# Low parts of two mixers' weights made by GpSimd and an accumulating transfer, in an order chosen from six rules

## The chip, the cores and the metric

One core of a Trainium2 chip runs the whole kernel. The metric is the device time of one execution in microseconds. TensorE (PE in the profile) multiplies, VectorE (DVE), ScalarE (ACT) and GpSimd (POOL) work on tiles, and SyncE (SP) issues the loads.

## The reference

Two layers of a transformer over 512 tokens of width 1024, batch 1, in float32. Each layer has a mixer, a cross attention to 256 memory tokens and a gated feed-forward, each behind a norm and followed by another norm that is added to the stream.

```python
for layer in range(2):
    h = rms_norm(x, g[0])
    y = even_mixer(h, ...) if layer % 2 == 0 else diff_mixer(h, ...)
    x = x + rms_norm(y, g[1])
    y = memory_cross_attention(rms_norm(x, g[2]), mem_n, wq, wk, wv, wo)
    x = x + rms_norm(y, g[3])
    y = swiglu(rms_norm(x, g[4]), wg, wu, wd)
    x = x + rms_norm(y, g[5])
```

The mixer of layer 0 has 8 heads with a forget gate ("fox") and 8 heads in two groups that add compressed, selected and windowed attention ("nsa"). The mixer of layer 1 has 8 differential heads of width 128. Each mixer begins with projections of `h` by one wide weight matrix and ends with an output matrix.

## The kernel before

Every product that needs float32 precision is made from three products in the faster type float32r: each operand is split into a rounded part `hi` and the rest `lo`, and `mm` adds hi*hi, hi*lo and lo*hi in PSUM. So each weight that comes from memory is split once before its use. `wunit` does that for 128x1024 elements: SP loads 512 KB into one of 3 `raw` buffers, then `split` lets ScalarE write `hi` (a copy that rounds) and VectorE write `lo` (raw minus hi). `hi` and `lo` lie in 8 buffers called `w`, four pairs. A unit with `rows` has a gain for each row multiplied in and goes another way (`wq`, and the keys and values of the memory).

The mixers: `mixer0` projects values, keys and compressed keys for all four blocks of 128 tokens, then works through the fox heads in pairs (`fox_proj`, `fox_units`), the queries of each nsa group (`nsa_q`), the compressed scores (`nsa_cmp`, products with 32 columns) and the two groups' attention (`nsa_units`). `mixer1` projects two heads at a time (`proj`: values, queries, keys, each by two units of weights) beside the attention of the two heads before. `last_heads` runs beside the last group of heads in both layers: `first_heads` multiplies the first six 128-row pieces of the heads' output by the output matrix (two times three units, one for each 512 columns, and two more units kept for the last two pieces), and `chain` takes each block of 128 tokens through the last two pieces, the norm, the memory attention with `wq` and `wo`, and the next norm. `wo` is two units, which need two of the four pairs. Softmax rows are scaled by GpSimd (`tensor_scalar`), and GpSimd computes the power of each norm on one column.

Nothing is issued where the code stands. Each call goes to a `Plan`, which notes the instruction, its tiles and a price in nanoseconds. `order` then runs a list scheduler forward through all instructions (`forward`), computes from the result how late each may be (`backward`), takes that as the new priorities, and repeats. The run with the shortest modelled end gives the order in which every engine's queue is written, the loads on SP included. `ALPHA` and `BETA` say when an engine should wait for a more urgent instruction that is soon ready, and `AHEAD` says how far an instruction may take a buffer out of turn.

Of the kernel before, what the change touches and what calls it, by code (L numbers as in the profile page):

```python
# [11 lines left out]
F32 = mybir.dt.float32  # L12
F32R = mybir.dt.float32r
I32 = mybir.dt.int32
AF = mybir.ActivationFunctionType
ALU = mybir.AluOpType
# [3 lines left out]
P = 128  # L20
# [15 lines left out]
KA = 6  # L36
PLAIN = 2
HALF_ROWS = 115
ROWS = slice(0, DH), slice(DH, P)
ORDER = 0, 4, 5, 6, 7, 1, 8, 9, 10, 11, 12, 13, 2, 3  # L40
FILL0, FILL1, STAGE, LATE = 0.0, 1.2, 2.0, 30
# [48 lines left out]
class Plan:  # L90
# [3 lines left out]
    LAT = dict(tt=0, ts=197, tv=230, tg=200, st=265, ss=160, sv=145, sg=170, vt=235, vs=198, vv=127, vg=203,  # L94
               gt=190, gs=190, gv=60, gg=110)
    BLOCK = 8
    ROUNDS = 14
    WINDOW = 4096 / 1.2
    FREE = 150.0
    NEAR, FEW = 10000.0, 12  # L100
    AHEAD, EARLY, RING = 50000.0, 60000.0, 8
    ALPHA, BETA = 1.0, 2.0

    def __init__(self, nc):
        self.nc = nc
# [73 lines left out]
    def price(self, eng, method, args, kw, aps):  # L179
        n = max([self.free(a) for a in aps] + [1])  # L180
        if method == "dma_start":
            size = 1
            for _, k in aps[0].ap:
                size *= k
            return size * 4 / 360.0
        if eng == "tensor":
            if method == "transpose":
                return 109.0
            c = self.free(args[2]) / 2.4
            return max(25.0, (13.0 if c > 100 else 6.5) + (c if args[2].dtype == F32R else 4 * c))  # L190
        half = HALF_ROWS if eng in ("scalar", "vector") and n > 100 and aps[0].ap[0][1] == DH else 0
        if eng == "scalar":
            extra = sum(isinstance(kw.get(k), bass.AP) for k in ("bias", "scale", "accum_out"))
            return (52 if aps[1].space == PSUM else 95) + 0.83 * n + 93 * extra + half
        if eng == "vector":
            psum = any(a.space == bass.MemoryType.PSUM for a in aps)
            n = n + 62 * sum(isinstance(v, bass.AP) and self.free(v) == 1 for v in args[2:3])
            if method == "reciprocal":
                return 60 + 8 * n
            if method in ("tensor_copy", "tensor_scalar", "memset") and not psum:  # L200
                return 65 + 0.52 * n
            return 65 + 1.04 * n + half
        if eng == "gpsimd":
            if method == "tensor_tensor":
                return 260 + 200 * n
            if method == "memset":
                return 30 + 0.84 * n
            return (322 if len(aps) > 3 else 222) + 0.84 * n
        raise ValueError(method)

    def order(self):
        ops = self.ops
        n = len(ops)
        self.eng = [o["eng"] for o in ops]
        self.succ = [[] for _ in range(n)]
        for i, o in enumerate(ops):
            for j in o["deps"]:
                self.succ[j].append(i)
        best = None
        prio = [float(o["prio"]) for o in ops]  # L220
        for _ in range(self.ROUNDS):
            for i, o in enumerate(ops):
                prio[o["group"]] = min(prio[o["group"]], prio[i])
            prio = [prio[o["group"]] for o in ops]
            for k, o in enumerate(self.firsts):
                prio[o["group"]] = k - 1e9
            r = self.forward(prio, self.AHEAD - best[0] if best else math.inf)
            if best is None or r[0] < best[0]:
                best = r
            prio = self.backward(r)  # L230
        self.span, self.at, self.fin, out = best[:4]
        return out

    def backward(self, run):

        span, at, fin, out, reuse = run
        ops, eng, n = self.ops, self.eng, len(self.ops)
        pred = [list(o["deps"]) for o in ops]
        for j, i in reuse:
            pred[i].append(j)  # L240
        left = [0] * n
        for p in pred:
            for j in p:
                left[j] += 1
        engines = ("tensor", "vector", "scalar", "gpsimd", "sync")
        ready = {e: [] for e in engines}
        busy = {e: 0.0 for e in engines}
        ev = [(0.0, i, i) for i in range(n) if not left[i]]
        heapq.heapify(ev)
        at2 = [0.0] * n  # L250
        late = [0.0] * n
        seq = n
        while ev:
            now = ev[0][0]
            while ev and ev[0][0] <= now + 1e-9:
                i = heapq.heappop(ev)[2]
                if i >= 0:
                    heapq.heappush(ready[eng[i]], (-fin[i], i))
            for e in engines:
                h = ready[e]  # L260
                while h and busy[e] <= now + 1e-9:
                    i = heapq.heappop(h)[1]
                    cost = ops[i]["cost"]
                    end = now + cost
                    if ops[i]["dma"]:
                        end += 2000
                    late[i] = -end
                    busy[e] = now + (60 if ops[i]["dma"] and e != "sync" else cost)
                    heapq.heappush(ev, (busy[e], seq, -1))
                    seq += 1  # L270
                    for j in pred[i]:
                        left[j] -= 1
                        f = eng[j]
                        at2[j] = max(at2[j], end + self.LAT.get(f[0] + e[0], 100.0))
                        if not left[j]:
                            heapq.heappush(ev, (max(at2[j], now), j, j))
        return late

    def forward(self, prio, far):

        ops, eng, succ = self.ops, self.eng, self.succ
# [111 lines left out]
        while done < n:  # L393
# [21 lines left out]
            while again:  # L415
                again = False
                for e, heap in ready.items():
                    while heap and busy[e] <= now + 1e-9:
# [12 lines left out]
                        cost = o["cost"]  # L431
                        if o["dma"]:
                            at[i] = now
                            busy[e] = now + 60
                            gen = max(gen, now + 100, ring.pop(0)) + 460
                            dma = max(dma, gen + 640) + cost
                            fin = dma + 950
                            ring.append(fin)
                        else:
                            if e == "tensor":  # L440
                                while now >= (window + 1) * self.WINDOW:
                                    share = worked / self.WINDOW
                                    warm = share > 0.82 or warm and share > 0.42
                                    window, worked = window + 1, 0.0
                                begin = max(now, begin + o["load"] * (1 if warm else 2))
                                if not warm:
                                    cost *= 2
                                worked += cost
                                at[i] = begin
                            else:  # L450
                                at[i] = now
                            busy[e] = fin = at[i] + cost
# [20 lines left out]
class Trunk:  # L473
    def __init__(self, ctx, tc, a, out):
        self.tc, self.a, self.out = tc, a, out
        self.nc = Plan(tc.nc)
        self.sb = ctx.enter_context(tc.tile_pool(name="sb", bufs=1))
        self.ps = ctx.enter_context(tc.tile_pool(name="ps", bufs=1, space=PSUM))
        self.loads = []


    def bank(self):
# [15 lines left out]
    def wunit(self, pieces, n, where=None, rows=None, raw=None):  # L498

        nc = self.nc  # L500
        raw = raw or self.tile([P, 1024], F32, "raw", 3)
        for dst, src in pieces:
            self.loads.append(nc.sync.dma_start(dst(raw), src))
        if where is None:
            hi, lo = [self.tile([P, 1024], F32R, "w", 8) for k in ("hi", "lo")]
        else:
            hi, lo = where()
        if rows is None:
            self.split(hi[:, :n], lo[:, :n], raw[:, :n])
        else:  # L510
            c = n // len(rows)
            for k, f in enumerate(rows):
                s = slice(k * c, (k + 1) * c)
                self.split(hi[:, s], lo[:, s], raw[:, s], f)
        return hi, lo
# [499 lines left out]
    def ffn(self, l, x, ops):  # L1015
# [2 lines left out]
        blocks = {"A11": [t[:, 0:4, 0:256] for t in hT], "A12": [t[:, 4:8, 0:256] for t in hT],  # L1018
                  "A22": [t[:, 4:8, 256:512] for t in hT], "S3": [t[:, 0:4, 256:512] for t in hT],
                  "S1": S[1], "S2": S[2], "S4": S[4]}  # L1020
        groups = [list(range(c, min(c + 3, NCH))) for c in range(0, NCH - 1, 3)]
        groups[-1].append(NCH - 1)
        acts = {}
# [114 lines left out]
    def mixer0(self, x0):  # L1138
# [78 lines left out]
        kcT, kcL, vcBD = self.compress(zst)  # L1217

        oS = self.oS_tiles(2)
        fox, nq, pc = {}, {}, {}  # L1220

        def fox_proj(p):
# [297 lines left out]
    def mixer1(self, x, blocks):  # L1520
# [70 lines left out]
            proj_qk(0, wf, tb, 1)  # L1591
        late.pop()()
        oS = self.oS_tiles(NT)

        def subln(ops, dst):

# [127 lines left out]
```

## Time and profile before

| | |
|---|---|
| median of 3 runs | 1386.26 us (1384.96 to 1386.47) |
| profiled execution | 1385.17 us |
| its span, first to last instruction | 1383.4 us |
| busy: TensorE, VectorE, ScalarE, GpSimd | 1352.8, 1114.9, 861.1, 200.0 us |
| transfers | 132.29 MB, all issued by SP |

Busy time of an engine is the time in which at least one of its instructions was under way; matmuls overlap in the pipeline, so a busy TensorE is one that never ran dry. All instructions stand under one source line (L470, where the planner issues them), so rows are told apart by their tiles: `w<-raw,w` is the making of a low part from `raw` and the high part.

### The profile page before, as it was taken

What the parts mean: (1) busy time and instruction counts of PE and PEld (TensorE: products, weight loads), DVE (VectorE), ACT (ScalarE), POOL (GpSimd) and SP (SyncE); (2) the same over time, 40 slices, a digit from 0 to 9 for tenths busy, and PEclk for the clock granted to TensorE, in tenths of its full rate; (3) what the DMA queues carried; (4) which work ended last, traced back from release to release, by engine and by line L of the source; (5) the groups of instructions that cost most, each with busy time, mean ns of one, the idle gap of its engine ahead of it and who ended that gap; (6) DMA issues with size and microseconds to landing.
All of it is one profiled execution on the core that took longest, in us unless ns stands there. A gap on an engine that the chain in (4) does not pass through costs nothing.

```text
span 1383.4 us, 25460 instructions
## 1 busy us (share of the span) xinstructions
PE 1352.8 (98%) x9443; PEld 1247.4 (90%) x9443; DVE 1114.9 (81%) x2485; ACT 861.1 (62%) x1954; POOL 200.0 (14%) x307
## 2 busy tenths in 40 slices
PE   7999999999899999999999999999999999999998
PEld 6788998888799999999989999988889999999997
DVE  6767899589897887788786788795999788778876
ACT  5758879588766355345455778795886545434542
POOL 2102223343300000000010132321430000000000
PEclk9999999999999999999999999999999999999999
DMA  7252112412234343323432231253223424332431
GB/s 224 67 154 63 32 32 77 137 47 77 62 96 119 92 122 107 93 80 119 128 116 62 77 106 49 77 169 106 77 62 92 122 85 130 95 104 77 123 107 61
DMA packets 150444, 132.29 MB, mean 96 GB/s; under 512 B 6928, under 2 KB 134096, under 8 KB 150320
## 3 DMA queue, kind: packets, MB, share of 16 engines
q1 hardware_dynamic: 150320, 130.67, 31.0%
q8 instruction: 74, 1.21, 0.4%
q14 instruction: 50, 0.41, 0.1%
HBM read 126.26 MB, written 4.19 MB: 94 GB/s over the span
## 4 chain that ended last, share of the span: by engine, by line
PE 84%; DVE 8%; ACT 2%; issue 2%; DMA 2%; POOL 1%; SPq 0%; POOLq 0%; DVEq 0%; ACTq 0%
PE ps L470 84%; DVE q L470 2%; DVE u L470 1%; DVE x L470 1%; DVE w L470 1%; POOL c L470 1%; DVE pt L470 1%; ACT q L470 1%; DMA raw<-in_ffn_wu_dram 1%; ACT junk L470 1%; DVE c L470 1%; DVE hTlo L470 1%; DMA x<-in_x_dram 0%; DMA raw<-in_od_w_in_dram 0%; ACT u L470 0%
## 5 line engine op out<-in xcount | busy, mean ns | idle before, releaser
L470 PE MATMUL ps<-hThi,w 128*128 128x256 f32 (+1 forms) x1664 | 338.4, 292 | 1.7 <-ACT hThi L470 1.2
L470 PE MATMUL ps<-w,hThi 128*128 128x256 f32 (+2 forms) x1280 | 282.9, 316 | 1.6 <-ACT hThi L470 1.6
L470 PEld LDWEIGHTS ps<-hThi,w 128*128 128x128 f32 x1664 | 272.1, 192 | 8.8 <-ACT hThi L470 2.1
L470 PE MATMUL ps<-hTlo,w 128*128 128x256 f32 (+1 forms) x832 | 242.2, 292 | 2.4 <-DVE hTlo L470 2.4
L470 PE MATMUL ps<-pt,u 128*128 128x512 f32 (+3 forms) x1126 | 231.4, 339 | 0.4 <-DVE pt L470 0.3
L470 PEld LDWEIGHTS ps<-w,hThi 128*128 128x128 f32 x1280 | 210.4, 192 | 14.3 <-ACT hThi L470 2.3
L470 PEld LDWEIGHTS ps<-pt,u 128*128 128x128 f32 (+1 forms) x1126 | 173.9, 174 | 28.5 <-DVE pt L470 1.0
L470 PE MATMUL ps<-w,hTlo 128*128 128x256 f32 (+2 forms) x640 | 199.4, 313 | 0.0
L470 DVE TENSOR_TENSOR w<-raw,w 128x512 fp32r<-128x512 f32 (+2 forms) x193 | 170.3, 887 | 31.6 <-ACT w L470 27.4
L470 PE MATMUL ps<-u,w 128*128 128x256 f32 x1440 | 192.9, 283 | 0.4 <-DVE ps L470 0.4
L470 ACT ACTIVATE w<-raw 128x512 fp32r<-128x512 f32 (+2 forms) x193 | 148.5, 786 | 68.8 <-DMA raw<-in_ffn_wg_dram 24.7
L470 ACT ACTIVATE q<-ps 128x256 f32<-128x256 f32 (+5 forms) x282 | 118.3, 428 | 112.1 <-PE ps L470 96.3
L470 PE MATMUL ps<-u 128*128 128x512 f32 (+4 forms) x806 | 185.8, 348 | 1.1 <-ACT u L470 0.6
L470 PEld LDWEIGHTS ps<-u,w 128*128 128x128 f32 x1440 | 181.8, 192 | 1.4 <-DVE ps L470 0.9
L470 DVE TENSOR_TENSOR u<-ps,u 128x512 f32<-128x512 f32 (+6 forms) x278 | 149.6, 545 | 39.8 <-PE ps L470 20.8
L470 PEld LDWEIGHTS ps<-hTlo,w 128*128 128x128 f32 x832 | 159.3, 192 | 6.1 <-DVE hTlo L470 3.2
L470 ACT ACTIVATE u<-ps 64x256 fp32r<-64x256 f32 (+5 forms) x277 | 120.5, 442 | 51.1 <-PE ps L470 47.6
L470 PEld LDWEIGHTS ps<-u 128*128 128x128 f32 (+1 forms) x806 | 129.4, 184 | 19.8 <-ACT u L470 1.2
L470 POOL TENSOR_TENSOR c<-c,mhalf 128x1 f32<-128x1 f32 (+1 forms) x68 | 60.9, 897 | 511.5 <-DVE c L470 502.6
L470 ACT ACTIVATE w<-q 128x512 fp32r<-128x512 f32 x160 | 99.9, 629 | 48.4 <-PE ps L470 22.7
L470 PEld LDWEIGHTS ps<-w,hTlo 128*128 128x128 f32 x640 | 122.4, 192 | 6.6 <-DVE hTlo L470 0.2
L470 DVE TENSOR_TENSOR w<-q,w 128x512 fp32r<-128x512 f32 x160 | 107.9, 686 | 21.2 <-ACT w L470 20.5
(153 smaller groups left out, 1917.6 us busy)
## 6 DMA issues: line engine op xcount, KB each, us to landing
raw<-in_ffn_wg_dram SPq DMA_DIRECT2D x44, 512.0 KB
raw<-in_ffn_wu_dram SPq DMA_DIRECT2D x44, 512.0 KB
raw<-in_ffn_wd_dram SPq DMA_DIRECT2D x44, 512.0 KB
raw<-in_od_w_in_dram SPq DMA_DIRECT2D x24, 512.0 KB
raw<-in_ev_w_in_dram SPq DMA_DIRECT2D x16, 512.0 KB
u<-in_sandwich_g_dram SPq DMA_DIRECT2D x10, 512.0 KB
x<-in_x_dram SPq DMA_DIRECT2D x8, 512.0 KB
raw<-in_ev_w_out_dram SPq DMA_DIRECT2D x8, 512.0 KB
```

The lines of the kernel that those rows point to most:

```text
L470: getattr(getattr(self.nc, self.eng[i]), method)(*args, **kw)
```

## The change

The planner's constants, prices and search, and one way of making low parts:

- `wunit` has a third way, taken where `rows` is None and a flag `mixing` is set: ScalarE writes `hi` as before; GpSimd writes raw times -1 into `lo`, which rounds, so that it is minus `hi`; then GpSimd issues a transfer from `raw` to `lo` that adds to what is there. VectorE has no part in it.
- The flag is set in `mixer0` after the compression and in `mixer1` after the first projections, and taken back at the start of `ffn`.
- An issue of a transfer on GpSimd holds that engine for `SOFT_DMA` = 1000 ns in the plan, and an accumulating transfer counts three times its size.
- A matmul with under 120 columns and a 128-column stationary operand is priced at 109 ns.
- `order` makes 10 rounds under each of six triples of `ALPHA`, `BETA`, `AHEAD` (60 in all) where it made 14 under one, starting from the program's order each time.

```diff
+SOFT_DMA = 1000
...
-    ROUNDS = 14
+    ROUNDS = 10
...
-    AHEAD, EARLY, RING = 50000.0, 60000.0, 8
-    ALPHA, BETA = 1.0, 2.0
+    EARLY, RING = 60000.0, 8
+
+    RULES = (1.0, 2.0, 5e4), (0.5, 2.0, 5e4), (0.5, 4.0, 5e4), (1.0, 4.0, 8e4), (1.0, 2.0, 8e4), (1.5, 4.0, 3.5e4)
...
-            return size * 4 / 360.0
+            return size * 4 / 360.0 * (3 if "accum_op" in kw else 1)
...
             c = self.free(args[2]) / 2.4
+            if c < 50 and self.free(args[1]) == P:
+                return 109.0
...
-        prio = [float(o["prio"]) for o in ops]
-        for _ in range(self.ROUNDS):
+        for turn in range(self.ROUNDS * len(self.RULES)):
+            if turn % self.ROUNDS == 0:
+                prio = [float(o["prio"]) for o in ops]
+                self.ALPHA, self.BETA, self.AHEAD = self.RULES[turn // self.ROUNDS]
+                far = math.inf
...
-            r = self.forward(prio, self.AHEAD - best[0] if best else math.inf)
+            r = self.forward(prio, far)
             if best is None or r[0] < best[0]:
                 best = r
+            far = self.AHEAD - r[0]
             prio = self.backward(r)
...
-                    busy[e] = now + (60 if ops[i]["dma"] and e != "sync" else cost)
+                    busy[e] = now + (SOFT_DMA if ops[i]["dma"] and e != "sync" else cost)
...
-                            busy[e] = now + 60
+                            busy[e] = now + (60 if e == "sync" else SOFT_DMA)
...
+        self.mixing = False
...
-        if rows is None:
+        if rows is None and self.mixing:
+            nc.scalar.activation(hi[:, :n], raw[:, :n], AF.Copy)
+            nc.gpsimd.tensor_scalar(lo[:, :n], raw[:, :n], -1.0, 1.0, op0=ALU.mult, op1=ALU.mult)
+            nc.gpsimd.dma_start(lo[:, :n].bitcast(F32), raw[:, :n], accum_op=ALU.add)
+        elif rows is None:
             self.split(hi[:, :n], lo[:, :n], raw[:, :n])
```

## Rows read from the trace of the kernel before

**Rows 1.** The page: busy time and share, and a DMA queue.

```profile
PE 1352.8 (98%) x9443; PEld 1247.4 (90%) x9443; DVE 1114.9 (81%) x2485; ACT 861.1 (62%) x1954; POOL 200.0 (14%) x307
...
q1 hardware_dynamic: 150320, 130.67, 31.0%
```

**Rows 2.** Busy time by stretch: length, engines (instructions), granted clock, DMA share, GB/s.

```profile
0.00:105.00 105.00, 95.89 (x543) 80.88 (x544) 68.01 (x189) 66.76 (x134) 15.74 (x39) 1.00 0.51 146
...
175.00:245.00 70.00, 68.44 (x512) 62.78 (x511) 65.37 (x245) 56.95 (x156) 22.60 (x34) 0.98 0.19 61
245.00:315.00 70.00, 69.72 (x432) 60.61 (x431) 49.43 (x153) 49.34 (x125) 24.58 (x34) 1.00 0.29 98
315.00:385.00 70.00, 63.84 (x491) 56.34 (x490) 62.48 (x119) 56.57 (x149) 21.91 (x31) 1.00 0.18 54
...
770.00:910.00 140.00, 139.67 (x1149) 137.56 (x1148) 115.03 (x390) 106.14 (x302) 37.46 (x57) 1.00 0.23 69
...
980.00:1060.00 80.00, 75.86 (x602) 69.92 (x601) 75.36 (x137) 65.14 (x164) 22.74 (x30) 1.00 0.23 71
```

**Rows 3.** The chain of waits, pieces: start us, us, what.

```profile
236.23 1.62 DVE w L470
...
383.58 303.23 PE ps L470 x2133
...
693.83 5.65 DMA raw<-in_od_w_in_dram
...
997.66 1.91 POOL q L470 x2
...
1004.52 1.15 DVE w L470
...
1059.53 4.62 DMA raw<-in_ffn_wu_dram
```

**Rows 4.** Groups of VectorE by shape: count, busy us, mean ns, idle before.

```profile
L470 DVE TENSOR_TENSOR w<-raw,w 128x1024 fp32r<-128x1024 f32 x70 | 85.4, 1231 | 11.7 <-ACT w L470 7.5 <-PE ps L470 3.3
```

**Rows 5.** Timeline of TensorE at the compressed scores: start us, us, what.

```profile
191.10 0.26 PE L470 MATMUL ps<-kcT,u 128*128 128x32 f32 x1
191.21 0.26 PE L470 MATMUL ps<-kcL,u 128*128 128x32 f32 x1
```

**Rows 6.** Groups of GpSimd by shape.

```profile
L470 POOL MEMSET u<- 128x1024 f32 x21 | 19.6, 962 | 372.9 <-PE ps L470 311.1 <-ACT u L470 61.7
...
L470 POOL TENSOR_SCALAR q<-q,c 128x512 f32<-128x512 f32 x8 | 6.1, 759 | 3.2 <-DVE c L470 3.2
...
L470 POOL TENSOR_SCALAR q<-q,c 128x128 f32<-128x128 f32 x8 | 3.0, 373 | 31.0 <-DVE c L470 30.9
```

**Rows 7.** GpSimd instructions on tile q: ns minimum/median/maximum.

```profile
L470 POOL TENSOR_SCALAR q<-q,c x64: 371/478/1796, 106.2 to 1013.8; 128x256 f32<-128x256 f32 x40, 128x128 f32<-128x128 f32 x8, 128x384 f32<-128x384 f32 x8, 128x512 f32<-128x512 f32 x8
```

**Rows 8.** Timeline of all engines around wo of layer 0.

```profile
336.96 1.47 PE L470 MATMUL ps<-w,u 128*128 128x256 f32 x10
...
337.16 3.54 POOL L470 TENSOR_SCALAR q<-q,c 128x256 f32<-128x256 f32 x6 [2.14 <-DVE c L470]
...
338.12 0.38 SPq L470 DMA_DIRECT2D raw<-in_ffn_wu_dram  x1
...
345.92 1.67 PEld L470 LDWEIGHTS ps<-w,q 128*128 128x128 f32 x8 [0.29 <-DVE q L470]
```

**Rows 9.** Timeline of TensorE around wo of layer 1.

```profile
995.04 3.12 PE L470 MATMUL ps<-w,u 128*128 128x256 f32 x24
...
1006.33 0.45 PE L470 MATMUL ps<-w,q 128*128 128x512 f32 x1
```

**Rows 10.** Timelines of VectorE and TensorE at the output weights of layer 0.

```profile
262.99 2.36 DVE L470 TENSOR_TENSOR w<-raw,w 128x1024 fp32r<-128x1024 f32 x2
...
265.21 0.71 PE L470 MATMUL ps<-w,hThi 128*128 128x512 f32 x2
```

More of the change, by code (lines that the diff above doesn't have):

```diff
@@ L1020, in ffn @@
                   "S1": S[1], "S2": S[2], "S4": S[4]}
+        self.mixing = False
         groups = [list(range(c, min(c + 3, NCH))) for c in range(0, NCH - 1, 3)]
@@ L1219, in mixer0 @@
         oS = self.oS_tiles(2)
+        self.mixing = True
         fox, nq, pc = {}, {}, {}
@@ L1593, in mixer1 @@
         oS = self.oS_tiles(NT)
+        self.mixing = True
         def subln(ops, dst):
```

## The prediction

> **What bounds the kernel now.** I read the page first. TensorE is busy for 1352.8 of 1383.4 us [rows 1], so 30.6 us is all that better feeding could give back unless its own work shrinks, and this change takes no product away. Next came the busy time by stretch, to see where the 30.6 us lie [rows 2]. The start (0 to 105) has 105.00 - 95.89 = 9.1, waiting for the first loads. The feed-forward of layer 0 is one unbroken TensorE run of 303 us on the chain [rows 3]. The middle of mixer 1 (770 to 910) has 0.3 in 140 us. What the mixers lose sits in three places: 1.6 around the compressed scores (175 to 245), 6.2 where the last heads, the memory attention and the norms of layer 0 run through (315 to 385), 4.1 at the same place of layer 1 (980 to 1060). There VectorE is at 65.4 of 70, 62.5 of 70 and 75.4 of 80. The clock was granted in full (2.4 GHz) nearly everywhere, so the clock gives nothing back. The chain of waits says the same [rows 3]: long TensorE runs, broken in those three places by short pieces of VectorE, ScalarE and GpSimd work. A split of a weight is rarely among them: two of the 50 that change are pieces of the chain, 1.62 us at 236 and 1.15 us at 1004.5.
>
> **The change part by part.** *Removed from VectorE.* By the code 22 units of mixer 0 (8 of the fox projections, 4 of the queries, 8 of the output weights, 2 of wo) and 28 of mixer 1 (18, 8, 2) take the new way. Each drops one subtraction over 128x1024, 1231 ns [rows 4]: 50 x 1.23 = 61.5 us of VectorE. Most of it goes where TensorE has no idle time: 245 to 315 lost 0.3 us with VectorE at 49.4 of 70, 770 to 910 lost 0.3 [rows 2]. There the removal is worth nothing, since TensorE's own work covers it; were that cover gone, as in the three bound places, a split would cost its 1.23. So I count the pieces on the chain, 1.62 + 1.15 = 2.8 us. The bounds are 0 (another VectorE instruction steps into the place, since the engine is near full there) and about 3.7: at 997.66 two GpSimd normalisations on the chain took 1.91 us where the median of their kind is 0.48 each [rows 3, 7], and a split was running then. **Relief: -2.8.**
>
> *Added to GpSimd.* Each unit gets one copy with a sign over 128x1024. No row has it. Scaling 128x128 takes 373 ns and 128x512 takes 759 [rows 6], 1.0 ns a column, so 759 + 512 x 1.0 = 1.27 us; a 1024-column memset, which reads nothing, took 0.96 and is the lower end. Then GpSimd issues a transfer. Nothing of the kind stands in the trace; SP needs 0.38 us for one of its own [rows 8], the longest GpSimd row of rows 7 is 1.80. I take the planner's new constant, 1.0, which lies between. That is 50 x 2.27 = 113 us more on an engine that had 20 to 25 us of work in 70. It fits, but it stands in front of the softmax normalisations and the one-column powers of the norms, which share its queue, and transposes on TensorE wait for those.
>
> A GpSimd row shows a second cost: the same scaling took from 371 up to 1796 ns [rows 7], and the split at 236 took 1.62 instead of 1.23 while a GpSimd scaling ran. The Trainium skill has a rule for this (SBUF — State Buffer, Who interferes with whom): a VectorE instruction with two SBUF inputs and a GpSimd instruction that reads SBUF exclude each other, and the second one stands still. By that rule, the trace agrees; it speaks against the change, for a subtraction on VectorE becomes a reader on GpSimd that can hold up every other subtraction there.
>
> *Added to the DMA engines.* 50 accumulating transfers of 512 KB within SBUF. All loads together kept the 16 engines for 31.0% of 1383.4 us for 130.67 MB [rows 1], so 0.524 MB holds them for 1.72 us. Loads that the chain waited for took 4.62 and 5.65 us from issue to landing [rows 3]. I take 4.6 to 5.7 us as the lower end; accumulating also reads its target, and the planner now prices the movement three times as high, so the upper end is 5.7 + 2 x 1.72 = 9.1. Against ScalarE's copy and the subtraction (about 2.3 us after the buffers come free), the low part is ready 1.27 + 1.0 + 4.6 = 6.9 to 11.4 us after. The Trainium skill (DMA: Bandwidth & Descriptors, Anatomy of one DMA) gives about 2.0 us plus the bytes at 436 GB/s for a transfer issued by GpSimd, an estimate of 3.2 us here; no run yet shows it, and by it the sum below would end some 1.5 us lower.
>
> Who waits for that? Where weights are fetched a step ahead, nobody, I take it. Two places per layer work just in time, because eight w buffers are four pairs. First, wo: its second pair comes free only when the last query projection ends. In layer 0 that is 336.96 + 1.47 = 338.4; GpSimd is busy with six normalisations until 340.7; then 1.27 + 1.0 + 4.6 (to 9.1) gives 347.6 to 352.1, where the product wants it at 345.9 [rows 8]: 1.7 to 6.2 us late, or 2.3 less if the copy is put ahead of the normalisations. In layer 1 the pair is free at 998.2 and wanted at 1006.33 [rows 9]: copied at once it lands at 1005.1, 1.2 early; behind the two normalisations that end at 999.6 and with the dear transfer, 1010.9, 4.6 late. Other work fills part of it; I take 1 us for each layer. Second, the output weights of the second 512 columns: two units are split at 262.99 to 265.35 and used from 265.2 on [rows 10]; they would come 4 to 9 us later. Heads of attention are still open there and VectorE has room, so I take 0, with 8 a layer as the far end. The raw buffer is held longer too (three exist), so SP's next loads, the feed-forward's first, start some us later; one is issued at 338.1, far ahead of the unbroken run from 383.6 [rows 8, 3]. **Waits: +2.0**, bounds 0 and +10.8 from wo alone (6.2 + 4.6).
>
> *The order.* Sixty passes of the planner under six triples of constants replace fourteen under one. All engines' queues are written anew, SP's loads too. One price is mended: 64 score products with 32 columns, which the trace starts 0.11 us apart [rows 5], were priced at 25 ns and are now at 109, so 64 x 0.084 = 5.4 us of TensorE work in 175 to 245 that the old order didn't see. Bounds for a better order: 0, and the idle time of the shown stretches after the start, 1.6 + 0.3 + 6.2 + 0.3 + 4.1 = 12.5. A worse one is possible, since ten rounds replace fourteen under the old triple and the model judges, not the chip. I take the 1.6 of the stretch with the mended price and a third of the largest, 2.0: **-3.6.**
>
> **Sum.** 1383.4 - 2.8 + 2.0 - 3.6 = 1379.0 us of span. The profiled execution had 1385.17 - 1383.4 = 1.8 outside its span, so 1380.8; it lay 1.1 below the median of the runs shown (1386.26), so I forecast 1381.9, rounded to 1382.
>
> **The rivals.** *A, the forecast:* a small gain, 1377 to 1383.4. *B, hidden anyway:* 48 of the 50 subtractions were off the chain, the two others are replaced by the next VectorE instruction, or GpSimd's new readers hold VectorE up for as long as they free it; then -2.8 falls away, the order gives 1 or 2, wo costs as much: about 1386. For it speaks that TensorE is full where most of the work was removed; against it that the mended price and the search work without the relief. *C, slower:* the low part is late at wo. With the dear transfer behind the normalisations both layers pay, 6.2 + 4.6 = 10.8, against gains of 6.4: +4.4, about 1391. It decides from waits of 9.2 us in sum (gains of 6.4 plus 2.8). For it speaks the chain of layer 1, which runs through GpSimd and VectorE exactly there; against it that the planner knows the pair's release and prices the transfer dear. *D, a much better order:* most of the 12.5 come back, say 10, with the relief and hardly any wait: about 1373.5.
>
> **How the numbers follow.** Chances: A 0.43, B 0.22, C 0.23, D 0.12. About 0.2%, 2.8 us, is what a measurement of this kernel can tell from no change; so faster (below 1383.5) is A and D, 0.55, same is B, 0.22, slower is C, 0.23. The range, 1372 to 1392, takes in D's and C's times with the bounds of the wo wait and leaves about 2 in 10 outside (both output-weight waits in the open, or an order that the model misjudges).
>
> **What would show it.** Right: 50 fewer 128x1024 subtractions on VectorE (about 61 us of busy time gone), 50 scalings on GpSimd near 1.3 us, 50 transfers on a queue of their own that land in 5 to 9 us; TensorE's idle time in 175 to 245 and in the two late stretches down by 4 to 5 us in sum; no wait of TensorE for a w transfer over 2 us. Wrong: TensorE or its weight loads waiting for w's transfers at the output weights or wo; normalisations on GpSimd queued behind copies, with transposes waiting; an issue on GpSimd far above 1 us; or a late stretch that has merely moved its idle time to other instructions.

## The result and the profile after

The changed kernel took 1397.76 us (median of 4 runs, 1395.56 to 1400.39), the kernel before beside it 1386.37 (4 runs, 1384.96 to 1389.13). The ratio is 1.008 (95% interval 1.0067 to 1.0092): about 11 us slower. The forecast was 1382 with a range of 1372 to 1392, so it missed in sign, and the result lies outside the range. The profiled span grew from 1383.4 to 1393.8, by 10.4.

The page of the changed kernel answers to [rows 1]: busy time by engine, two DMA queues (packets, MB, share of 16 engines) and the new issue line (count, size, median us to landing).

```profile
PE 1357.7 (97%) x9443; PEld 1249.2 (90%) x9443; DVE 1079.3 (77%) x2435; ACT 859.1 (62%) x1954; POOL 283.4 (20%) x407
...
q1 hardware_dynamic: 150320, 130.67, 30.8%
q0 software_dynamic: 7200, 26.22, 10.4%
...
w<-raw POOLq DMA_DIRECT2D x48, 512.0 KB, 5.4
```

The change does what it says: VectorE has 50 instructions and 35.6 us less, GpSimd 100 instructions and 83.4 us more, and a queue of its own carries 26.22 MB. That VectorE lost only 35.6 of the 61.5 us counted is a first hint: added up one by one, its other instructions became about 20 us longer. TensorE makes the same 9443 products, but is busy 4.9 us longer and idle 36.1 us in place of 30.6.

GpSimd's groups by shape in the changed kernel, count, busy us, mean ns; two more of each kind, for other tiles, make 50.

```profile
L478 POOL TENSOR_SCALAR w<-raw 128x1024 fp32r<-128x1024 f32 x48 | 55.6, 1159 | 112.8 <-DMA raw<-in_ev_w_in_dram 51.4 <-PE ps L478 34.8 <-ACT u L478 11.0
L478 POOL DMA_DIRECT2D w<-raw x48 | 42.7, 890 | 14.4 <-POOL w L478 14.2 <-POOL q L478 0.2
```

Busy time by stretch in the changed kernel answers to [rows 2].

```profile
0.00:105.00 105.00, 91.60 (x502) 75.76 (x503) 61.84 (x176) 60.58 (x123) 26.12 (x49) 0.95 0.58 155
...
175.00:245.00 70.00, 68.70 (x521) 62.30 (x520) 65.14 (x250) 60.17 (x163) 29.66 (x41) 1.00 0.18 52
245.00:315.00 70.00, 70.00 (x446) 61.58 (x444) 42.37 (x147) 49.28 (x127) 31.85 (x46) 1.00 0.56 138
315.00:385.00 70.00, 66.26 (x513) 59.45 (x513) 64.18 (x123) 58.06 (x157) 27.41 (x37) 1.00 0.35 99
...
770.00:910.00 140.00, 139.36 (x1148) 137.51 (x1147) 109.31 (x368) 104.14 (x296) 60.45 (x86) 1.00 0.54 129
910.00:980.00 70.00, 68.48 (x358) 57.01 (x358) 40.51 (x112) 48.61 (x127) 30.54 (x43) 1.00 0.72 191
980.00:1060.00 80.00, 73.45 (x559) 66.47 (x558) 71.79 (x137) 63.96 (x168) 24.05 (x38) 0.98 0.31 87
```

Two stretches got worse. In the first 105 us TensorE idles 105 - 91.60 = 13.4 us where it idled 9.1 [rows 2], and the granted clock is 0.95. In 980 to 1060 it idles 6.6 where it idled 4.1, at 0.98. The stretch from 315 to 385 got better, idle 3.7 in place of 6.2. Finer windows of the changed kernel find the first loss:

```profile
85.00:90.00 5.00, 2.92 (x8) 1.15 (x8) 4.44 (x10) 2.83 (x6) 4.40 (x6) 0.76 1.11 243
90.00:95.00 5.00, 2.90 (x11) 2.51 (x12) 2.78 (x8) 1.05 (x6) 1.64 (x2) 0.50 1.02 164
95.00:100.00 5.00, 5.00 (x18) 3.97 (x17) 0.90 (x4) 0.65 (x3) 1.96 (x2) 0.72 1.09 286
```

The same windows of the kernel before:

```profile
85.00:90.00 5.00, 5.00 (x23) 4.06 (x22) 2.68 (x8) 3.09 (x6) 0.00 (x0) 1.00 0.87 239
90.00:95.00 5.00, 5.00 (x23) 3.75 (x23) 4.01 (x9) 3.46 (x8) 0.00 (x0) 1.00 0.45 124
95.00:100.00 5.00, 5.00 (x25) 4.16 (x24) 4.28 (x7) 4.89 (x9) 0.00 (x0) 1.00 0.48 127
```

TensorE is busy 2.9 of 5 us twice, and the clock falls from 2.4 to 1.2 GHz in the middle of it. The kernel before had 5.00 of 5 at full clock in all three. The idle time costs 4.2 us; the clock costs 2.92 x 0.24 + 2.90 x 0.50 + 5.00 x 0.28 = 3.6 us of TensorE work. Together that is 7.7 us.

Not all of it reaches the end. By 600.0 us, in the middle of the first feed-forward, the kernel before has begun 3974 products; the changed one has by 604.4, so it is 4.4 us behind there and has made up 3.3. The unbroken run of products that ends both kernels begins at 1110.13 us before and at 1120.11 after, 10.0 later. So layer 1 loses another 5.6 us, nearly all of it in 910 to 1060: 3.4 us more idle time and 1.5 for the clock of 0.98.

What is at 85? The compression has just ended its products, and its tail runs through small steps on VectorE and ScalarE before the next transposes. In the timeline only products of the first fox projections stand between these steps. TensorE's timeline in the changed kernel (start, us, what, idle before and releaser):

```profile
84.87 0.50 PE L478 MATMUL ps<-hThi,w 128*128 128x512 f32 x1
85.21 0.40 PE L478 MATMUL ps<-hTlo,w 128*128 128x512 f32 x1
86.07 0.43 PE L478 MATMUL ps<-q,ones 1*66 1x128 f32 x2 [0.46 <-ACT q L478]
86.43 0.50 PE L478 MATMUL ps<-hThi,w 128*128 128x512 f32 x1
86.76 0.40 PE L478 MATMUL ps<-hTlo,w 128*128 128x512 f32 x1
87.95 0.79 PE L478 MATMUL ps<-hThi,w 128*128 128x512 f32 x1 [0.79 <-ACT w L478]
88.55 0.63 PE L478 MATMUL ps<-hTlo,w 128*128 128x512 f32 x1
91.78 0.48 PE L478 MATMUL ps<-ident,q 66*128 66x66 f32 x2 [2.60 <-DVE q L478]
...
93.89 1.20 PE L478 MATMUL ps<-hThi,w 128*128 128x512 f32 x2
```

Three units in turn get two single products, those with the high part of the weights, and stop: the third needs the low part. The third unit's products, at 87.95, are already longer (0.79 and 0.63 us in place of 0.50 and 0.40): the clock fell behind idle times of 0.46 and 0.79 us. In the kernel before the same place is an unbroken run of such products, and it is this cover that is missing: the tail itself ends no later than before, its last 66x128 step at 91.8 us where it was 94.9. GpSimd's timeline in the changed kernel shows when the low parts were made:

```profile
82.49 1.33 POOL L478 TENSOR_SCALAR w<-raw 128x1024 fp32r<-128x1024 f32 x1 [40.90 <-DMA raw<-in_ev_w_in_dram]
84.16 1.05 POOL L478 DMA_DIRECT2D w<-raw  x1 [0.33 <-POOL w L478]
84.94 1.37 POOL L478 TENSOR_SCALAR w<-raw 128x1024 fp32r<-128x1024 f32 x1
86.62 0.89 POOL L478 DMA_DIRECT2D w<-raw  x1 [0.31 <-POOL w L478]
87.24 1.36 POOL L478 TENSOR_SCALAR w<-raw 128x1024 fp32r<-128x1024 f32 x1
88.90 0.88 POOL L478 DMA_DIRECT2D w<-raw  x1 [0.30 <-POOL w L478]
```

These three transfers took 5.2, 5.4 and 6.8 us from issue to landing, so the low parts come at 89.4, 92.0 and 95.7. Yet the first product that needs one begins at 93.89, 4.5 us after the first has landed: the plan had put the transposes of 91.78 ahead of it in TensorE's queue, and these wait for VectorE. In the whole trace no wait of TensorE is put down to a transfer into `w` (in experiments 2 and 11 a single one is, of 1.5 and 1.6 us, in 900 to 1060). So the low parts cost time here by the order that the plan made for them, with a movement priced at three times its size, and not by a wait for their landing. Whether a lower price would have put their products first, no run shows.

Each transfer also holds its raw buffer until it lands. SP's timeline shows 4 loads of weights in 78 to 93, where the kernel before (second line) has 6:

```profile
78.67 13.88 SPq L478 DMA_DIRECT2D raw<-in_ev_w_in_dram  x4
78.91 14.39 SPq L470 DMA_DIRECT2D raw<-in_ev_w_in_dram  x6
```

The longest idle time of TensorE, 2.60 us, though, is put down to VectorE, to the compression's own tail. VectorE's timeline there shows a second loss: steps of 66x128, which take 0.22 to 0.29 us when alone, last over a microsecond while GpSimd copies or clears a buffer.

```profile
85.05 0.29 DVE L478 TENSOR_TENSOR q<-ps,q 66x128 f32<-66x128 f32 x1 [2.13 <-PE ps L478]
85.37 1.09 DVE L478 TENSOR_TENSOR q<-q 66x128 f32<-66x128 f32 x1
...
86.83 1.91 DVE L478 TENSOR_TENSOR q<-q 66x128 f32<-66x128 f32 x2
...
90.11 1.68 DVE L478 TENSOR_SCALAR q<-q 66x128 f32<-66x128 f32 x2
```

The first reads a PSUM tile and is not stretched; the next has both inputs in SBUF and ends with GpSimd's copy, at 86.5 against 86.3. So there are two suspects at one place: the low parts are **late**, by their landing or by their place in the plan, and GpSimd's copies **hold** VectorE.

### The profile page after: what moved, and what is told of

Read it like the earlier page. It is cut to its first block, busy times and chain, and to the rows that moved or that the text cites. A ratio compares the mean times of both kernels' runs of the same rounds, so it can differ in the third digit from the quotient of the medians.

```text
span 1393.8 us, 25605 instructions
## 1 busy us (share of the span) xinstructions
PE 1357.7 (97%) x9443; PEld 1249.2 (90%) x9443; DVE 1079.3 (77%) x2435; ACT 859.1 (62%) x1954; POOL 283.4 (20%) x407
## 3 DMA queue, kind: packets, MB, share of 16 engines
q0 software_dynamic: 7200, 26.22, 10.4%
## 4 chain that ended last, share of the span: by engine, by line
PE 82%; DVE 10%; ACT 3%; issue 2%; DMA 2%; POOL 1%; SPq 0%; POOLq 0%; DVEq 0%; ACTq 0%
PE ps L478 82%; DVE q L478 3%; DVE u L478 2%; DVE x L478 1%; DVE pt L478 1%; DVE w L478 1%; POOL c L478 1%; ACT q L478 1%; DVE c L478 1%; ACT junk L478 1%; DMA raw<-in_ffn_wu_dram 0%; ACT u L478 0%; DMA x<-in_x_dram 0%; DVE hTlo L478 0%; ACT pt L478 0%
## 5 line engine op out<-in xcount | busy, mean ns | idle before, releaser
L478 POOL TENSOR_TENSOR c<-c,mhalf 128x1 f32<-128x1 f32 (+1 forms) x68 | 54.1, 798 | 480.3 <-DVE c L478 480.3
L478 ACT ACTIVATE u<-ps 64x256 fp32r<-64x256 f32 (+6 forms) x277 | 120.3, 443 | 47.5 <-PE ps L478 43.6
L478 DVE TENSOR_TENSOR w<-raw,w 128x512 fp32r<-128x512 f32 (+2 forms) x145 | 111.8, 773 | 25.7 <-ACT w L478 24.3
```

The lines of the kernel that those rows point to most:

```text
L478: getattr(getattr(self.nc, self.eng[i]), method)(*args, **kw)
```

## The experiments

Lines of diffs stand against the changed kernel. The planner writes all orders anew for each kernel, so a difference can hold some of that too. The kernel before ran beside each, with medians from 1385.86 to 1387.21.

**1. The search alone.** The flag is never set, so all low parts come from VectorE; the prices and the six rules stay.

```diff
-        self.mixing = True
+        self.mixing = False
```

> The changed kernel with its flag never set: VectorE makes every low part as before, while the planner keeps the six rule triples, the 60 rounds and the mended price. Theory 1 (the low parts that land late cost the time, above all at the first fox projections, 85 to 94 us of the changed kernel, where TensorE has nothing else ready): this kernel is free of it, so 1380 to 1389 us. Theory 2 (the six-rule search picks an order that the chip runs worse): it is as slow as the changed kernel, 1394 to 1400. TensorE's idle time in 0 to 105 should be back near 9 us by theory 1 (13.4 in the changed kernel).

Measured: 1385.55 us, ratio 1.0 (0.999 to 1.0011). The new search and the mended price gain and lose nothing that these runs can tell.

**2. The low parts alone.** The old search (14 rounds, one triple, no price of 109 ns) with the new low parts.

```diff
-    ROUNDS = 10
+    ROUNDS = 14
...
-            if c < 50 and self.free(args[1]) == P:
-                return 109.0
```

> The other half: the low parts of the mixers by GpSimd and the accumulating transfer, with their prices in the plan, but the search of the kernel before (14 rounds, one triple) and no mended price for the 32-column products. Theory 1: as slow as the changed kernel, 1394 to 1402 us, with the same gap at the first fox projections. Theory 2: near the kernel before, 1384 to 1389.

Measured: 1398.9 us, 1.0083 (1.0068 to 1.0098). The whole loss comes with the low parts, and the gap is at the same place in this order too: TensorE is busy 2.88 us in 85 to 90, at a clock of 0.77.

**3. The first pair back on VectorE.** The flag is set behind the first fox projections: 2 units of 50 return, 48 stay.

```diff
-        self.mixing = True
         fox, nq, pc = {}, {}, {}
...
         drain(fox_proj(0))
+        self.mixing = True
```

> The changed kernel with one part undone: the two units of the first fox pair are split by VectorE again; the other 48 units keep the new way. Theory 1: most of the loss goes, 1386 to 1391 us, and TensorE's idle time in 0 to 105 is back near 9 us with the clock granted in full at 85 to 100; what stays above the kernel before is what the last heads of layer 1 lose. Theory 3 (GpSimd's copies and issues get in the way of the softmax and norms all over the mixers, by the shared port or its queue): it hardly helps, 1393 to 1398, because 48 of 50 units still go that way.

Measured: 1385.76 us, 0.9993 (0.9985 to 1.0002). Undoing two units takes off the whole loss. In part that is its order: the units of layer 1 go the new way as in the changed kernel, but TensorE is busy 67.88 + 76.17 = 144.1 us in 910 to 1060, where the changed one has 141.9 and the kernel before 145.3. The windows of this kernel show TensorE nearly full at full clock where the changed one had its gap, though the transfers run here as well:

```profile
85.00:90.00 5.00, 4.75 (x23) 3.52 (x22) 3.97 (x6) 2.51 (x7) 1.95 (x2) 1.00 0.81 220
90.00:95.00 5.00, 4.92 (x24) 3.66 (x23) 2.12 (x8) 4.96 (x10) 3.60 (x5) 1.00 1.10 243
```

**4. The last heads back on VectorE.** The flag is taken back at the start of `last_heads` in both layers (20 units: output weights and wo).

```diff
         step = 8.0 / n
+        self.mixing = False
```

> The changed kernel with the output weights and wo (20 units) split by VectorE again; the fox, query and differential projections (30 units) keep the new way. Theory 1 with its second place (powers of the norms and late wo in 910 to 1060): 2 to 4 us of the loss go, 1393 to 1396 us, and the gap at the first fox projections stays. My prediction's rival C put the whole loss at wo: by it this kernel is back at 1384 to 1389.

Measured: 1392.91 us, 1.0049 (1.0036 to 1.0063). TensorE's busy time is 69.60 in 910 to 980 and 75.43 in 980 to 1060, close to before; the gap at 85 stays (2.74 of 5 us). So the last heads hold a second loss of 4 to 5 us in the change's order.

**5. The first pair alone.** The reverse of experiment 3: only the first pair (2 units) by the new way.

```diff
         drain(fox_proj(0))
+        self.mixing = False
...
-        self.mixing = True
```

> The opposite of the third experiment: only the two units of the first fox pair go the new way, the other 48 low parts are made by VectorE. If those two units cost the loss by themselves wherever they stand, 1392 to 1398 us. If the loss needs that no fox unit is ready while the compression's chain of small steps runs (two pairs late, nothing to fill TensorE with), the second pair's products fill the gap here: 1384 to 1388, and TensorE's idle time in 0 to 105 is near 9 us. After the third experiment I expect the second.

Measured: 1385.25 us, 0.999 (0.9981 to 0.9999). The same late low parts at the same place cost nothing once the second pair, made by VectorE, has products ready: TensorE is busy 4.42 us in 85 to 90 and 5.00 in 90 to 95. GpSimd's copies hold steps of the tail here as well (0.81 us for one, 1.63 for two). So it isn't the first pair's lateness by itself that costs, nor the hold, but the lack of any unit that is ready.

**6. A plain transfer.** GpSimd issues the same transfer without the addition. The price of the movement stays three times the size.

```diff
-            nc.gpsimd.dma_start(lo[:, :n].bitcast(F32), raw[:, :n], accum_op=ALU.add)
+            nc.gpsimd.dma_start(lo[:, :n].bitcast(F32), raw[:, :n])
```

> The changed kernel with a plain transfer in place of the accumulating one, priced in the plan as the accumulating one is, so that only the transfer's kind differs. It leaves out the addition: the low part becomes the raw weight. If accumulating is what makes the low part late, the transfer lands 1.5 us or more sooner than the 5.4 of the changed kernel, and the gap at the first fox projections shrinks: 1390 to 1394 us. If it is the way by GpSimd at all (copy, issue, fixed cost of a transfer, loads in the same engines), the landing moves by under 1 us and the time stays 1394 to 1400.

Measured: 1388.84 us, 1.0014 (1.0006 to 1.0023). The page of this kernel, queue and issue line:

```profile
q0 software_dynamic: 7200, 26.22, 5.1%
...
w<-raw POOLq DMA_DIRECT2D x48, 512.0 KB, 3.3
```

With a landing 2.1 us sooner, four fifths of the loss are gone. The landing isn't the only difference, since the issue takes GpSimd 0.59 us in place of 0.89 and the movement half as much of the DMA engines. The gap is shorter, not gone: TensorE is busy 2.57 and 4.63 us in 85 to 90 and 90 to 95. The first transfer, issued at 83.90, lands after 3.9 us, at 87.8, but under the same price its product stands behind the transposes of 89.73 again and begins at 91.74.

**7. Neither end.** Experiments 3 and 4 together: 28 units by the new way, in the middle of the mixers.

> The third and fourth experiments together: the first fox pair and all of the last heads (22 units) by VectorE, the other 28 by GpSimd and transfers, which still takes 34 us of work from VectorE. If the relief of VectorE is worth anything where the low parts are in time, 1380 to 1384 us, faster than the kernel before. If relief is worth nothing there because TensorE is full, 1384 to 1387.

Measured: 1389.77 us, 1.002 (1.0008 to 1.0031). A miss: neither known loss is left, and yet it is no faster than before. The windows of this kernel show a clock at half for 10 us, behind an idle time of 0.23 us, in a stretch of compressed scores that lost nothing like it before:

```profile
170.00:175.00 5.00, 4.77 (x42) 4.60 (x41) 4.82 (x12) 4.54 (x10) 1.25 (x2) 0.97 0.01 2
175.00:180.00 5.00, 5.00 (x25) 5.00 (x25) 3.97 (x19) 1.17 (x3) 0.00 (x0) 0.50 0.00 0
180.00:185.00 5.00, 5.00 (x26) 5.00 (x25) 1.88 (x12) 0.31 (x1) 0.00 (x0) 0.50 0.00 2
```

That is 5 us of TensorE work, about the loss in this profiled execution. It doesn't come in every run: the five of twelve with a mean clock of 0.997 or more took 1385.8 to 1387.9 us, the seven at 0.993 to 0.995 took 1389.7 to 1392.6. So even where it doesn't come, these runs show no gain from the relief. Whether the new way brought the fall or the order did is not settled; the idle time before it is put down to ScalarE (tile `pt`, the turned softmax rows), not to a weight.

**8. The subtraction on GpSimd.** One instruction, raw minus high part, and no transfer: no late landing, but 2.4 us of GpSimd work for each unit.

```diff
-            nc.gpsimd.tensor_scalar(lo[:, :n], raw[:, :n], -1.0, 1.0, op0=ALU.mult, op1=ALU.mult)
-            nc.gpsimd.dma_start(lo[:, :n].bitcast(F32), raw[:, :n], accum_op=ALU.add)
+            nc.gpsimd.tensor_tensor(lo[:, :n], raw[:, :n], hi[:, :n].bitcast(F32), op=ALU.subtract)
```

> The same 50 low parts, made by one subtraction on GpSimd (raw minus the high part), with no transfer and no copy; the plan prices it at 2.45 us. VectorE is relieved as in the changed kernel, but the low part is ready about 2.5 us after the high part and not 7 to 8 us after the load. If lateness is the cause, 1382 to 1388 us. If GpSimd's work in the way of softmax and norms is the cause (theory 3), it keeps GpSimd for as long as copy and issue together and reads two operands, so 1392 to 1398.

Measured: 1409.47 us, 1.0158 (1.0142 to 1.0173), the slowest of all, and a miss for lateness as the only cause. There is no gap at 85 here (95.27 of 105 us busy); most of the loss lies in mixer 1's attention, where TensorE is busy 133.08 of 140 us in 770 to 910, at a clock of 0.95. The timeline of that kernel, GpSimd's row and VectorE's:

```profile
868.33 4.71 POOL L478 TENSOR_TENSOR w<-raw,w 128x1024 fp32r<-128x1024 f32 x2
```

```profile
866.18 0.42 DVE L478 TENSOR_TENSOR rope<-q,cs 128x64 f32<-128x64 f32 x3
...
868.34 4.84 DVE L478 TENSOR_TENSOR rope<-q,cs 128x64 f32<-128x64 f32 x3 [0.50 <-ACT q L478]
873.22 0.22 DVE L478 TENSOR_TENSOR q<-rope 128x64 f32<-128x64 f32 x1
```

Three steps of a rotation (64 or 32 columns each), 0.42 us two microseconds earlier, start with GpSimd's two subtractions and end with them. The longest single one took 0.38 us before, 1.83 in the changed kernel, 2.47 here. This hold is what the Trainium skill describes (SBUF — State Buffer, Who interferes with whom): a VectorE instruction with two inputs in SBUF contends with a GpSimd instruction that reads SBUF, for ports that they share under an exclusive lock. The trace agrees.

**9. The last heads alone.** The flag is set at the start of `last_heads` and nowhere else: 20 units.

> Only the weights used beside the last heads of the two layers (output weights and wo, 20 units) are made the new way; the 30 units before them go by VectorE. Theory 1 (low parts late at the first fox projections): TensorE in 0 to 105 is busy about 95 us at full clock as before, and the time is that of before, 1384 to 1388. If the last heads have a loss of their own, the 4.9 us that came back when these 20 units were taken out of the changed kernel should come on top of before: 1390 to 1392, with TensorE's busy time in 910 to 1060 some 2 to 3 us under the 145.3 of before. If that loss stood only in the one order, as the kernel with the first pair by VectorE lets one think, nothing of it is here.

Measured: 1387.19 us, 1.0012 (1.0003 to 1.0022). TensorE is busy 67.96 + 74.84 = 142.8 us in 910 to 1060 where it was 145.3, so the last heads lose 2.5 us, of which 1.7 are left by the ratio, less than the 4 to 5 of experiment 4. The two losses don't add up; each kernel's order deals with them anew.

**10. wo by VectorE.** The 4 units of wo return, 46 stay.

```diff
+            self.mixing = False
             c["wo"] = [self.w_cols(a["ca_wo"][l], 0, 1, 1024, k) for k in range(2)]
+            self.mixing = True
```

> The changed kernel, but the low parts of wo (4 of the 50 units) by VectorE. Rival C of the prediction (the low part late at wo): most of the loss goes, 1387 to 1390. If the late parts at the fox projections carry most and the last heads' share comes from wo: about 1393, as with all 20 units of the last heads taken out. If it comes from the output weights or from GpSimd's queue: 1396 to 1399, no change. In all three the gap of TensorE at 85 to 95 stays, with about 3 of 5 us busy and a lower clock.

Measured: 1394.98 us, 1.0068 (1.0055 to 1.0081). That is 1.7 us under the change by the ratios, with intervals that overlap. But the ratio hides more: in 910 to 1060 TensorE is busy 69.83 + 74.39 = 144.2 us, against 141.9 in the changed kernel and 145.3 before, while layer 0 does worse in this order (3974 products begun by 608.6 us, against 604.4). So wo, the place of rival C, carries some 2 us of idle time in layer 1; how much of the total it carries, these orders don't tell apart.

**11. Late, but without the hold.** In the first four units (pairs 0 and 1) ScalarE writes minus the rounded weights; the transfer stays.

```diff
+            if self.early:
+                nc.scalar.activation(lo[:, :n], raw[:, :n], AF.Copy, scale=-1.0)
+            else:
+                nc.gpsimd.tensor_scalar(lo[:, :n], raw[:, :n], -1.0, 1.0, op0=ALU.mult, op1=ALU.mult)
```

> The changed kernel, but in the first four units (fox projections of pairs 0 and 1) ScalarE writes minus the rounded weights instead of GpSimd; the accumulating transfer stays, and the other 46 units are as in the change. It takes two causes of the gap at 85 to 95 apart, both found in the trace of the changed kernel. Lateness (copy, issue and a landing of 5.4 us before the product can run): nothing improves, TensorE is busy about 3 of 5 us in the two windows, 1394 to 1398. Hold (GpSimd's copies make the compression's small VectorE steps of 0.29 us last 1.1 to 1.3): the steps are back at 0.29 to 0.5, the gap is 3 us shorter, 1388 to 1392.

Measured: 1394.88 us, 1.0062 (1.0045 to 1.0079). VectorE's timeline of this kernel has the first steps back at their own length:

```profile
85.54 0.29 DVE L478 TENSOR_TENSOR q<-q 66x128 f32<-66x128 f32 x1 [0.23 <-DVE q L478]
...
87.23 0.48 DVE L478 TENSOR_TENSOR q<-q 66x128 f32<-66x128 f32 x2
...
90.34 1.88 DVE L478 COPY q<-q 128x128 f32<-128x128 f32 x2 [0.72 <-ACT q L478]
```

The gap stays all the same (3.22 and 3.53 us busy in the two windows, clock 0.91 and 0.50). So GpSimd's copies aren't needed for a gap here. It doesn't show that lateness makes it, either. The edit puts more on ScalarE, which is busy 4.95 of 5 us there, and a clearing of a buffer by GpSimd still holds VectorE (1.88 us for two copies that take 0.36 elsewhere). TensorE's waits in 80 to 100 are put down to ScalarE's `w` (1.4 us) and `q` (0.7) and to VectorE's `q` (1.3), none to a transfer.

**12. The hold, but not late.** VectorE makes all low parts as before, and GpSimd then copies each raw buffer onto itself, 50 copies of the same size that change nothing; no transfers.

```diff
+            self.split(hi[:, :n], lo[:, :n], raw[:, :n])
+            nc.gpsimd.tensor_scalar(raw[:, :n], raw[:, :n], 1.0, 1.0, op0=ALU.mult, op1=ALU.mult)
```

> All 50 low parts by VectorE as before, and after each one a GpSimd copy of the raw buffer onto itself with the change's size (128x1024, times 1), which does nothing for the result and holds the raw buffer longer; no transfers. So GpSimd's copies are there without late low parts. Lateness: the second pair's products are there to fill, 1384 to 1389. Hold: the copies stretch VectorE's steps and sit in GpSimd's queue before the normalisations, with VectorE's 61 us back on top: 1390 to 1398.

Measured: 1390.27 us, 1.0025 (1.0013 to 1.0037). TensorE has no gap at 85 to 95 (5.00 and 5.00 of 5 us), though two steps of the compression last 1.04 and 0.96 us; the loss lies later. Windows of this kernel:

```profile
770.00:910.00 140.00, 138.18 (x1138) 135.93 (x1137) 116.93 (x386) 102.87 (x293) 50.44 (x74) 1.00 0.25 76
...
980.00:1060.00 80.00, 74.17 (x581) 68.01 (x580) 74.34 (x137) 63.95 (x163) 24.00 (x35) 0.98 0.22 67
```

GpSimd's copies cost 3.5 us by themselves, spread over the places where VectorE is busiest. The raw buffers are also held longer here, which the run doesn't take apart.

## Why the prediction was wrong

The step that failed is **Waits**, in the words "Where weights are fetched a step ahead, nobody, I take it". I looked for late low parts by one sign alone, w buffers that come free just in time, and so found wo and the output weights. The first fox projections need no such search: the flag is set at the end of the compression, they are the first units to take the new way, and their loads have only just landed. The sign that I gave for being right, no wait of TensorE for a `w` transfer over 2 us, held in the changed kernel, and it was slower all the same: the plan let TensorE wait for other work. Where I had entered nothing, the runs showed a gap of 4.2 us at 85 to 95 and 3.6 us more for the clock behind it. I had read the first 105 us as "waiting for the first loads" and not looked inside. A look at 78 to 95 in the trace before would have shown 66x128 steps on VectorE beside an unbroken run of fox products, which was the cover for the compression's tail. The rule that I wrote down myself, name the work that hides a cost, was applied to the subtractions removed and not to the tail that the projections hide.

- *Copy, issue, landing.* Forecast 1.27, 1.0 and 4.6 to 9.1 us; measured 1.16, 0.89 and 5.4. These were right. So was the latency: 82.5 to 89.4 for the first unit is 6.9 us, the lower end of the 6.9 to 11.4.
- *Load on the DMA engines.* 10.4% of 1393.8 us for 50 transfers is 2.9 us of all 16 engines each, between 1.72 and three times that. In 85 to 100 their share is 1.02 to 1.11, with loads and transfers together.
- *wo, +2.0.* About that much idle time in layer 1 (experiment 10), its share of the total open. Rival C had the right sign and, for most of the loss, the wrong place; the changed kernel's trace has no wait for a transfer there, those of experiments 2 and 11 one of 1.5 and 1.6 us in layer 1, far from 10.8.
- *The clock.* I wrote that it gives nothing back, and didn't ask what a new gap would take. It cost 3.6 us beside 4.2 us of idle time.
- *The order, -3.6.* Nothing that can be told (experiment 1). Shown idle time was no evidence that another search would fill it.
- *Relief, -2.8.* No gain in the end: with 48 of 50 units moved and the gap avoided, 0.9993 (0.9985 to 1.0002) in experiment 3, although VectorE is 33 us less busy there. That is what rival B forecast for the relief. Its condition that GpSimd's readers hold VectorE for as long as they free it isn't met, since about 20 of some 60 us come back as longer instructions; that TensorE is full where most of the work went fits. Experiment 12 prices the copies at 3.5 us against a relief of 2.8; that the two cancel is an estimate, not shown by a run.
- *The hold.* I named it, with a row for it, and entered nothing in the sum. The row mixes four widths, so its shortest and its longest aren't the same scaling; still, one of 128x256 took 1796 ns where the median of all is 478. Experiments 8 and 12 show that the hold costs.

What each loss is worth in the changed kernel: 7.7 us at 85 to 100 by the windows, of which 3.3 are made up before the feed-forward, and 5.6 in layer 1. The gap needs that no product of the fox projections is ready in TensorE's queue (experiments 3 and 5 take it away by either pair; 8 and 12 have the hold without the gap). How much of it is the landing, how much the plan's price for it, and how much the hold that stretches the tail, no run isolates. The loss in layer 1 comes with the last heads (4) and depends on the order (3, 9). Undoing 2 units took off all of it, undoing 20 others 4 to 5 us: the parts are not additive. No version tried beats the kernel before by the 0.2% that a measurement can tell; the nearest is experiment 5 at 0.999.

## What to carry to other kernels

Before a producer is made slower, list every place where its first product is used after a change of stage, and ask what else the consumer could run there; a cover that consists of the same kind of work is lost together with it. Such a loss need not show as a wait for the late result: a planned queue may have put other work first, and then the wait carries that work's name. Moving an elementwise pass from VectorE to GpSimd isn't free even where GpSimd has room: count the small VectorE steps that can fall under each GpSimd instruction, at that instruction's full length. A gap of a few microseconds on TensorE may cost nearly twice its length, as here (3.6 us of clock behind 4.2 of idle time).

## What the runs showed of the hardware

- An accumulating transfer of 512 KB within SBUF, issued by GpSimd, takes 5.4 us to land (4.5 to 8.7), 2.9 us of all 16 DMA engines and 0.89 us of GpSimd for the issue. The plain one of the same size takes 3.3 us, 1.4 us of the engines (5.1% of 1389.0 us for 50) and 0.59 us.
- The prediction's sentence on the Trainium skill (DMA: Bandwidth & Descriptors, Anatomy of one DMA) had an estimate of 3.2 us: the plain transfer's median of 3.3 agrees, the accumulating one took 2.2 us more.
- GpSimd's subtraction of 128x1024 took 2.44 us against VectorE's 1.23, and a VectorE rotation of 64 columns stood still behind it for up to 2.47 us.
- The clock fell to 1.2 GHz behind idle times of 0.46 and 0.79 us in the changed kernel and of 0.23 us in experiment 7, and stayed at 2.4 in 315 to 385, where TensorE idled 3.7 us in all.
